# A layer kernel on one core: the side transfers of the first sweep move from SyncE's queue to GpSimd's, and the root of a block's rows from GpSimd to VectorE

## The chip, the cores and the metric

The kernel runs on one core of a Trainium2 chip. The metric is the device time of one execution in microseconds; of three executions the median counts: 2177.08 us (2176.64 to 2177.74). A second number is the span, from the first to the last instruction of one profiled execution.

## The reference

One layer over 4096 latent tokens of 1024 channels, with 256 context tokens ahead of them, all in float32:

```python
mod_lat = silu(c) @ w_mod + b_mod                 # shift, scale, gate
a_lat = rmsnorm(x, norm_g) * (1 + sc_l) + sh_l    # a_ctx likewise, from ctx and c_ctx
q, zf, zb, v, ga, u, ug, gb = split(a_lat @ w_in) # 8 groups of 512 columns
o   = hgrn2 forward(q, v, zf) + hgrn2 backward(q, v, zb)   # gated linear recurrence, 4 heads x 128
y   = silu(layernorm(conv31(u * sigmoid(ug)) + conv_b))    # half of it along rows, half along columns
out = concat(headnorm(o) * silu(ga), y * silu(gb)) @ w_out
result = rmsnorm(x + gt_l * out, final_norm_g)
```

f is lb + (1 - lb) * sigmoid(z), the key is 1 - f, and a state is S = f * S + k v^T per token. The states start from those at the end of the context.

## The kernel before, in words

The work goes through the tokens twice. The first sweep takes 16 blocks of 256 tokens in rising order: it projects q, zf, zb, v, u and ug, runs the forward recurrence and the convolution along rows, and stores what the backward recurrence needs. The second sweep goes down again and makes the gates, the convolution along columns, the backward recurrence and the output projection. The change is in the first sweep alone. Projections are done with float16 pairs, a high and a low half, in three passes of matmuls (PASSES), so TensorE has about 76 us of work in a block.

In a block `b` of the first sweep several generators are merged, each a sequence of steps: `hgrn` (the recurrence of the block), `row_conv`, the projections of this block and the next ones, `prep_rows` of block b+2, and the side work `side[b]` of blocks 1 to 11. The program's text gives the work in this merged order; a scheduler of the framework then sets the final order on each engine with a model of its own, so an edit in one place can move instructions elsewhere, and side work may stand in the block before the one that it is written for. Every engine takes its instructions in order: one that waits holds all behind it. The same holds for the DMAs that SyncE (SP) issues, and for those that GpSimd (POOL) issues.

`hgrn` in a block: five levels multiply keys and queries X by products of f (L763, L764 on VectorE), ScalarE copies km (L756), and TensorE makes the scores pl (L731). Then come two more growths, Q and H (L773, L774, each for two groups gi), with scores across (L784, L785). Then `split_keys` makes K: the high half on ScalarE (L560), the low half on VectorE (L561), and a DMA transpose of K into X on SP's queue (L562). There are two K buffers for four splits in a block. `keys_to_u` on TensorE reads the transposed keys (pu, L578); `forward` updates the state s_f (L583).

`prep_rows` of a block (two tiles of 128 rows): a load of x into xt (L258), the square sum on ScalarE (L261), L262, the root of the mean (`rsqrt`, L78 on VectorE, then L81 and three times L84 and L85 on GpSimd: L81 halves, each pair is one Newton step on a 128x1 tile), the scaling (L268, L270), the split in halves hl (L271 on ScalarE, L273 on VectorE), and two DMA transposes of hl into aT on SP's queue (L276).

The side work prepares the weights of the second sweep: `gate_rows` (loads wmt, L861), `scale_w2` (loads wst L885, squares L888), `split_w2` (load L897, halves L188 and L189, store of hl into w2d L900), `wo_scales` (loads L909, squares L911), `split_wo` (loads of gw L974 and L975, L979, halves L980 and L981, store of hl into wod L982). It shares its buffers with `prep_rows`: tag "xt" has two buffers, tag "A" (hl, junk, sqj, gacc) has one, so the halves of one piece of side work can't be written before the store, or the transposes, of the piece before have read theirs.

Of the kernel before, what the change touches and what calls it, by code (L numbers as in the profile page):

```python
# [19 lines left out]
P = 128  # L20
D = 1024
# [52 lines left out]
def rsqrt(nc, pool, out, v, n, tag, eng=None):  # L74

    eng = eng or nc.gpsimd
    y, t, h = out, pool.tile([P, n], F32, tag=tag + "t", name=tag + "t"), v
    nc.vector.tensor_scalar(y.bitcast(I32), v.bitcast(I32), -0.5, float(0x5F3759DF), ALU.mult, ALU.add)  # L78
    if n == 1:
        h = pool.tile([P, n], F32, tag=tag + "h", name=tag + "h")  # L80
        eng.tensor_scalar(h, v, -0.5, 0.0, ALU.mult, ALU.add)  # L81
    for _ in range(3):
        if n == 1:
            eng.tensor_scalar(t, y, y, h, ALU.mult, ALU.mult)  # L84
            eng.tensor_scalar(y, t, 1.5, y, ALU.add, ALU.mult)  # L85
        else:
            eng.tensor_tensor(t, y, y, ALU.mult)  # L87
            eng.tensor_tensor(t, t, v, ALU.mult)  # L88
            eng.tensor_scalar(t, t, -0.5, 1.5, ALU.mult, ALU.add)  # L89
            eng.tensor_tensor(y, y, t, ALU.mult)  # L90
# [8 lines left out]
def hymba_block(  # L99
# [3 lines left out]
    nc = tc.nc  # L103
    x, cx, out = x[0], cx[0], out[0]
    w_mod, w_in, w_out, conv_w = w_mod[0], w_in[0], w_out[0], conv_w[0]

    cp = ctx.enter_context(tc.tile_pool(name="cp", bufs=1))
    sm = ctx.enter_context(tc.tile_pool(name="sm", bufs=2))
# [33 lines left out]
    gtd = dr.tile([P, D], F32, tag="gtd", name="gtd")  # L142
    gsd = dr.tile([2, D], F32, tag="gsd", name="gsd")
    w2d = {g: [dr.tile([P, 2, 2 * 512], F16, tag=f"w2d{g}_{i}", name=f"w2d{g}_{i}") for i in range(4)] for g in (G_GA, G_GB)}
    wod = [dr.tile([P, 2, KC, 512], F16, tag=f"wod{n}", name=f"wod{n}") for n in range(2)]
# [20 lines left out]
    def group_scale(ssq, g):  # L166

        with tc.high_priority():
            tot = sm.tile([P, 1], F32, tag="tot", name="tot")
            nc.vector.tensor_reduce(tot, ssq, AX.X, ALU.add)  # L170
            pb = ps_lv.tile([P, 512], F32, tag="lv", name="pb")
            nc.tensor.matmul(pb[:, 0:1], ones, tot, start=True, stop=True)
            rw = rwall[:, g, :]
            tot2 = sm.tile([P, 1], F32, tag="tot2", name="tot2")
            nc.vector.tensor_copy(tot2, pb[:, 0:1])
            exponent(rw[:, 0:1], rw[:, 1:2], tot2)

    def evac_scale(g):
        for i in range(2):
            nc.vector.tensor_scalar(es[:, i, g : g + 1], rwall[:, g, 1:2], ra[:, i : i + 1], 2.0 ** -28, ALU.mult, ALU.mult)  # L180
# [10 lines left out]
    def win_rows(g, k, n):  # L191
        return w_in[k * P : (k + n) * P, 512 * g : 512 * g + 512].rearrange("(k p) n -> p k n", p=P)
# [4 lines left out]
    with ExitStack() as s1:  # L197
# [55 lines left out]
        def prep_rows(r0, aT):  # L253

            for i in range(2):
                t = e1.tile([P, D], F32, tag="xt", name="xt", bufs=2)
                hl = e1.tile([P, 2, D], F16, tag="A", name="hl")
                nc.sync.dma_start(t, x[r0 + i * P : r0 + (i + 1) * P, :])  # L258
                yield
                ssq = sm.tile([P, 1], F32, tag="xssq", name="xssq")  # L260
                nc.scalar.activation(hl[:, 0, :].bitcast(BF16), t, AF.Square, accum_out=ssq)  # L261
                nc.vector.tensor_scalar(ssq, ssq, 1.0 / D, EPS, ALU.mult, ALU.add)  # L262
                r = sm.tile([P, 1], F32, tag="xr", name="xr")
                rsqrt(nc, sm, r, ssq, 1, "xq")
                yield
                for sl in (slice(0, 512), slice(512, D)):
                    ts = t[:, sl]
                    nc.vector.scalar_tensor_tensor(ts, ts, r, gs[:, 0, sl], ALU.mult, ALU.mult)  # L268
                    yield
                    nc.vector.tensor_tensor(ts, ts, gs[:, 1, sl], ALU.add)  # L270
                    nc.scalar.copy(hl[:, 0, sl], ts)  # L271
                    yield
                    nc.vector.tensor_tensor(hl[:, 1, sl], ts, hl[:, 0, sl], ALU.subtract)  # L273
                    yield
                for j in range(2):
                    nc.sync.dma_start_transpose(aT[:, j, :, i * P : (i + 1) * P], hl[:, j, :])  # L276
# [105 lines left out]
        for r0, src in ((R_NG, norm_g[0]), (R_BM, b_mod[0]), (R_LB, lb_logits.rearrange("a b n -> (a b n)")),  # L382
                        (R_HG, hgrn_norm_g[0]), (R_CB, conv_b[0]), (R_LG, conv_ln_g[0]), (R_LBI, conv_ln_b[0])):
            n = src.shape[0] // P
# [471 lines left out]
        def gate_rows():  # L856

            acc = e1.tile([P, D], F32, tag="A", name="gacc")
            for k in range(KC):
                t = e1.tile([P, D], F32, tag="xt", name="wmt", bufs=2)  # L860
                nc.sync.dma_start(t, w_mod[k * P : (k + 1) * P, 2 * D : 3 * D])  # L861
                if k == 0:
                    nc.vector.tensor_scalar(acc, t, sc2[:, k, 0:1], None, ALU.mult)
                else:
                    nc.vector.scalar_tensor_tensor(acc, t, sc2[:, k, 0:1], acc, ALU.mult, ALU.add)
                yield
            bt = e1.tile([P, D], F32, tag="xt", name="bt", bufs=2)
            nc.sync.dma_start(bt, bass.AP(b_mod.tensor, b_mod.offset + 2 * D, [[0, P], [1, D]]))
            for j in range(2):
                sl = slice(512 * j, 512 * j + 512)  # L870
                pg = ps_o.tile([P, 512], F32, tag="o", name="pg")
                nc.tensor.matmul(pg, ones, acc[:, sl], start=True, stop=True)
                nc.vector.tensor_tensor(bt[:, sl], bt[:, sl], pg, ALU.add)
            nc.sync.dma_start(gtd, bt)
            nc.vector.tensor_reduce(gmx[:, 0:1], bt, AX.X, ALU.max)
            nc.vector.tensor_reduce(gmx[:, 1:2], bt, AX.X, ALU.min)
            yield

        def scale_w2(g):

            ssq = sm.tile([P, 8], F32, tag="ssq", name="ssq")
            for i in range(4):
                t = e1.tile([P, 2, 512], F32, tag="xt", name="wst", bufs=2)
                junk = e1.tile([P, 2, 512], BF16, tag="A", name="sqj")
                nc.sync.dma_start(t, win_rows(g, 2 * i, 2))  # L885
                yield
                yield
                nc.scalar.activation(junk, t, AF.Square, accum_out=ssq[:, i : i + 1])  # L888
                yield
            group_scale(ssq[:, 0:4], g)  # L890
            evac_scale(g)

        def split_w2(g, i):

            t = e1.tile([P, 2 * 512], F32, tag="xt", name="wst", bufs=2)
            hl = e1.tile([P, 2, 2 * 512], F16, tag="A", name="hl")
            nc.sync.dma_start(t.rearrange("p (k n) -> p k n", n=512), win_rows(g, 2 * i, 2))  # L897
            yield
            split_chunk(hl[:, 0, :], hl[:, 1, :], t, g)
            nc.sync.dma_start(w2d[g][i], hl)  # L900
            yield

        def wo_scales():

            ssq = sm.tile([P, 8], F32, tag="ssq", name="ssq")
            for k in range(KC):
                t = e1.tile([P, D], F32, tag="xt", name="wst", bufs=2)
                junk = e1.tile([P, D], BF16, tag="A", name="sqj")
                nc.sync.dma_start(t, w_out[k * P : (k + 1) * P, :])  # L909
                yield  # L910
                nc.scalar.activation(junk, t, AF.Square, accum_out=ssq[:, k : k + 1])  # L911
                yield
# [55 lines left out]
        def split_wo(k):  # L968

            for n in range(2):  # L970
                sl = slice(512 * n, 512 * n + 512)
                gw = e1.tile([P, 2, 512], F32, tag="xt", name="gw", bufs=2)
                hl = e1.tile([P, 2, 512], F16, tag="A", name="hl")
                nc.sync.dma_start(gw[:, 0, :], gtd[:, sl])  # L974
                nc.sync.dma_start(gw[:, 1, :], w_out[k * P : (k + 1) * P, sl])  # L975
                yield
                w = gw[:, 1, :]
                f = khg[:, k : k + 1] if k < 4 else kw[:, 1:2]
                nc.vector.scalar_tensor_tensor(w, w, f, gw[:, 0, :], ALU.mult, ALU.mult)  # L979
                nc.scalar.copy(hl[:, 0, :], w)  # L980
                nc.vector.tensor_tensor(hl[:, 1, :], w, hl[:, 0, :], ALU.subtract)  # L981
                nc.sync.dma_start(wod[n][:, :, k, :], hl)  # L982
                yield

        side = {1: [gate_rows()], 2: [scale_w2(G_GA), scale_w2(G_GB)]}
        for i in range(4):
            side[3 + i] = [split_w2(G_GA, i), split_w2(G_GB, i)]
            side[8 + i] = [split_wo(2 * i), split_wo(2 * i + 1)]
# [325 lines left out]
```

## Time and profile before

| | before |
|---|---|
| median of 3 executions | 2177.08 us |
| profiled execution, time | 2179.47 us |
| profiled execution, span | 2177.7 us |
| granted TensorE clock, mean | 0.981 |
| TensorE, VectorE, ScalarE, GpSimd busy | 2056.2, 1757.6, 1006.0, 371.6 us |
| side work's DMA issues on SP: wmt, bt, gtd, wst (in, out), w2d, gw (two), wod | 8, 1, 1, 16, 8, 8, 32, 16 |

The busy numbers are of the whole span. The first sweep's blocks lie between about 100 and 1410 us, and a block begins on a row of opd (the store of the forward result, L830). Block numbers below are those of the first opd row in a stretch: the stretch from 211.0 to 295.9 us holds what ends with the keys of block 1, the one to 375.5 those of block 2, and so on; block 12 ends at 1196.5. A wait in the trace is idle time of an engine, put down to what came last.

### The profile page before, as it was taken

Reading aid. Unit: us, or ns where it says so; the run is one execution under the profiler, and the core shown is the slowest. Engines: PE = TensorE matmul, PEld = TensorE weight load, DVE = VectorE, ACT = ScalarE, POOL = GpSimd, SP = SyncE. Lnnn points to the kernel's source line nnn. Section 1 sums busy time; section 2 is a strip of 40 time slices with the busy share of each in tenths; the row PEclk is TensorE's granted clock in tenths of the full one; section 3 lists DMA queues with packets and bytes.
Section 4 is the critical chain, followed back from the end, with each engine's and each line's share of the span. In section 5 each row is a group of like instructions: output and inputs, shape, how many; then the busy total and the mean of one; then the engine's idle time right before and its main releaser. Section 6 shows DMA issues by size and latency. Waiting matters only on the chain. (4 is left out here: it accounts for less than half of the span.)

```text
span 2177.7 us, 54464 instructions
## 1 busy us (share of the span) xinstructions
PE 2056.2 (94%) x22339; PEld 1517.2 (70%) x22339; DVE 1757.6 (81%) x4283; ACT 1006.0 (46%) x2326; POOL 371.6 (17%) x886
## 2 busy tenths in 40 slices
PE   6999999999998998999999999989999999999998
PEld 3777778778777887777788888655555555565664
DVE  5988877977975978978887975969999888888744
ACT  4944546445446445455445434433343333343343
POOL 1110101101101101101101100013433333333222
PEclk8999999999999999999999999989999999999999
DMA  9436155335235254253333225443332222333221
GB/s 363 136 90 161 60 151 161 69 113 130 71 113 144 74 145 138 63 161 114 74 108 63 52 55 156 152 155 102 107 107 93 97 98 92 120 120 115 97 78 59
DMA packets 222082, 247.96 MB, mean 114 GB/s; under 512 B 143652, under 2 KB 151672, under 8 KB 217864
## 3 DMA queue, kind: packets, MB, share of 16 engines
q1 hardware_dynamic: 221288, 240.19, 37.8%
q8 instruction: 175, 2.87, 0.6%
q0 software_dynamic: 544, 4.29, 0.5%
q14 instruction: 75, 0.61, 0.1%
HBM read 138.52 MB, written 72.36 MB: 97 GB/s over the span
## 5 line engine op out<-in xcount | busy, mean ns | idle before, releaser
L289 PEld LDWEIGHTS <-w 128*128 128x128 f16 x4704 | 456.2, 98 | 61.8 <-issue 3.6
L711 DVE SCALAR_TENSOR_TENSOR yr<-gu,convw,yr 128x224 f32<-128x224 f32 (+2 forms) x900 | 357.9, 445 | 0.0
L1116 DVE SCALAR_TENSOR_TENSOR ycs<-gu_all,convw,ycs 128x256 f32<-128x256 f32 (+2 forms) x828 | 345.3, 471 | 0.0
L289 PEld LDWEIGHTS <-pair 128*128 128x128 f16 x3168 | 308.2, 98 | 39.4 <-issue 0.6
L1220 PE MATMUL py<-wo,yh 128*128 128x512 f16 x1024 | 251.4, 381 | 2.9 <-ACT yh L1204 2.9
L289 PE MATMUL ps_z<-aT,pair 128*128 128x256 f16 x1632 | 190.8, 276 | 0.0
L289 PE MATMUL ps_z<-aT,w 128*128 128x256 f16 x1632 | 188.6, 274 | 1.9 <-DVE aT L247 1.4
L1083 PE MATMUL ps_gb<-aT,w 128*128 128x256 f16 x1536 | 187.7, 273 | 0.0
L81 POOL TENSOR_SCALAR xqh<-xssq 128x1 f32<-128x1 f32 x30 | 12.5, 416 | 1022.8 <-DVE xssq L262 1022.8
L300 PE MATMUL pv<-w,aT 128*128 128x512 f16 x816 | 184.4, 379 | 1.3 <-DVE gu L675 1.3
L1071 PE MATMUL ps_ga<-w,aT 128*128 128x512 f16 x768 | 182.1, 382 | 0.0
L289 PE MATMUL ps_u<-aT,w 128*128 128x256 f16 x1536 | 181.3, 274 | 0.2 <-ACT q L657 0.2
L756 ACT COPY km<-X 128x512 f32<-128x512 f32 x160 | 107.9, 675 | 156.1 <-DVE X L764 155.8
L289 PE MATMUL ps_g<-aT,w 128*128 128x256 f16 x1536 | 177.8, 273 | 0.6 <-ACT q L657 0.6
L1220 PEld LDWEIGHTS <-yh 128*128 128x128 f16 x1024 | 100.4, 98 | 108.5 <-ACT yh L1204 4.0
L289 PE MATMUL ps_q<-aT,pair 128*128 128x256 f16 x1536 | 173.3, 273 | 0.0
L1083 PEld LDWEIGHTS <-w 128*128 128x128 f16 x1536 | 150.1, 98 | 31.8
L300 PEld LDWEIGHTS <-aT 128*128 128x128 f16 x816 | 77.4, 98 | 88.2 <-issue 1.5
L1071 PEld LDWEIGHTS <-aT 128*128 128x128 f16 x768 | 75.5, 99 | 81.6 <-issue 2.5
L1220 PE MATMUL py<-wo,yl 128*128 128x512 f16 x512 | 129.6, 379 | 0.0
L1226 ACT ACTIVATE jk<-xr 128x512 bf16<-128x512 f32 x64 | 40.3, 629 | 184.7 <-DVE xr L1224 128.4
L319 ACT ACTIVATE f<-f,lbv,oml 128x128 f32<-128x128 f32 x272 | 112.9, 486 | 0.0
(308 smaller groups left out, 3301.5 us busy)
## 6 DMA issues: line engine op xcount, KB each, us to landing
xt<-in_x_dram SPq DMA_DIRECT2D x32, 512.0 KB, 4.3
xr<-in_x_dram SPq DMA_DIRECT2D x32, 512.0 KB, 3.6
out_dram<-xr SPq DMA_DIRECT2D x31, 512.0 KB, 2.6
aTd<-aT SPq DMA_DIRECT2D x14, 1024.0 KB, 5.1
aT<-aTd SPq DMA_DIRECT2D x14, 1024.0 KB, 5.2
wst<-in_w_in_dram SPq DMA_DIRECT2D x16, 512.0 KB, 4.3
qb<-qbd SPq DMA_DIRECT2D x32, 256.0 KB, 2.7
ub<-ubd SPq DMA_DIRECT2D x32, 256.0 KB, 2.7
```

The lines of the kernel that those rows point to most:

```text
L81: eng.tensor_scalar(h, v, -0.5, 0.0, ALU.mult, ALU.add)
L289: nc.tensor.matmul(ps[:, j, :], w[:, wi, k, (ct + j) * P : (ct + j + 1) * P], aT[:, ai, k, :], start=n == 0, stop=n == 23)
L300: nc.tensor.matmul(pv, aT[:, ai, k, i * P : (i + 1) * P], W[G_V][:, wi, k, :], start=n == 0, stop=n == 23)
L319: nc.scalar.activation(fa, fa, AF.Identity, scale=oml[:, d, ct + j : ct + j + 1], bias=lbv[:, d, ct + j : ct + j + 1])
L711: nc.vector.scalar_tensor_tensor(ar[i][:, :, lo:hi], gr[i][:, :, lo + dl : hi + dl], convw[:, i, j : j + 1], ar[i][:, :, lo:hi], ALU.mult, ...
L756: nc.scalar.copy(fap(km, 0, kd), fap(Xs[gi], 0, ks))
L1071: nc.tensor.matmul(ps, aT[:, ai, k, i * P : (i + 1) * P], Wa[:, wi, k, :], start=n == 0, stop=n == 23)
L1083: nc.tensor.matmul(ps[:, j, :], Wb[:, wi, k, (ct + j) * P : (ct + j + 1) * P], aT[:, ai, k, :], start=n == 0, stop=n == 23)
L1116: nc.vector.scalar_tensor_tensor(ya, gu_all[:, i, (lo + dl) * GW : (hi + dl) * GW], convw[:, 2 + i, j : j + 1], ya, ALU.mult, ALU.add)
L1220: nc.tensor.matmul(py, y[:, k // 4, k % 4, :], W2["o", nh][:, wi, k, :], start=n == 0, stop=n == 23)
L1226: nc.scalar.activation(junk, h[:, sl], AF.Square, accum_out=hs[:, nh : nh + 1])
```

## The change

The DMA issues of all side work go from `nc.sync` to `nc.gpsimd`, and the root in `prep_rows` is given VectorE as its engine. Buffers, generators and the merging stay as they are.

```diff
@@ prep_rows
-                rsqrt(nc, sm, r, ssq, 1, "xq")
+                rsqrt(nc, sm, r, ssq, 1, "xq", nc.vector)
@@ gate_rows (also bt and the store gtd)
-                nc.sync.dma_start(t, w_mod[k * P : (k + 1) * P, 2 * D : 3 * D])
+                nc.gpsimd.dma_start(t, w_mod[k * P : (k + 1) * P, 2 * D : 3 * D])
@@ scale_w2
-                nc.sync.dma_start(t, win_rows(g, 2 * i, 2))
+                nc.gpsimd.dma_start(t, win_rows(g, 2 * i, 2))
@@ split_w2 (also its load)
-            nc.sync.dma_start(w2d[g][i], hl)
+            nc.gpsimd.dma_start(w2d[g][i], hl)
@@ wo_scales
-                nc.sync.dma_start(t, w_out[k * P : (k + 1) * P, :])
+                nc.gpsimd.dma_start(t, w_out[k * P : (k + 1) * P, :])
@@ split_wo
-                nc.sync.dma_start(gw[:, 0, :], gtd[:, sl])
-                nc.sync.dma_start(gw[:, 1, :], w_out[k * P : (k + 1) * P, sl])
+                nc.gpsimd.dma_start(gw[:, 0, :], gtd[:, sl])
+                nc.gpsimd.dma_start(gw[:, 1, :], w_out[k * P : (k + 1) * P, sl])
...
-                nc.sync.dma_start(wod[n][:, :, k, :], hl)
+                nc.gpsimd.dma_start(wod[n][:, :, k, :], hl)
```

The function that the root calls takes the engine as its last argument:

```python
def rsqrt(nc, pool, out, v, n, tag, eng=None):
    eng = eng or nc.gpsimd
```

First place: VectorE at the end of block 4, from the Q growths (X with 16x32) over the two H growths (8x64) to the first key splits K; xt, xssq, xr and xqt belong to `prep_rows`. Before:

```order
801 L774 TENSOR_TENSOR X<-X,FL 128x16x32
802 L773 TENSOR_TENSOR X<-X,FL 128x16x32
803 L774 TENSOR_TENSOR X<-X,FL 128x16x32
804 L262 TENSOR_SCALAR xssq<-xssq 128x1
805 L78 TENSOR_SCALAR xr<-xssq 128x1
806 L773 TENSOR_TENSOR X<-X,FL 128x8x64
807 L774 TENSOR_TENSOR X<-X,FL 128x8x64
808 L268 SCALAR_TENSOR_TENSOR xt<-xt,xr,gs 128x512 x2
809 L773 TENSOR_TENSOR X<-X,FL 128x8x64
810 L774 TENSOR_TENSOR X<-X,FL 128x8x64
811 L270 TENSOR_TENSOR xt<-xt,gs 128x512
812 L561 SCALAR_TENSOR_TENSOR K<-X,K 128x512
```

The same place in the changed kernel, which begins with the second side split L189 of the block (before, both L189 stood ahead of the Q growths):

```order
915 L189 SCALAR_TENSOR_TENSOR hl<-wst,rwall,hl 128x1024
916 L773 TENSOR_TENSOR X<-X,FL 128x8x64
917 L774 TENSOR_TENSOR X<-X,FL 128x8x64
918 L773 TENSOR_TENSOR X<-X,FL 128x8x64
919 L774 TENSOR_TENSOR X<-X,FL 128x8x64
920 L561 SCALAR_TENSOR_TENSOR K<-X,K 128x512 x2
921 L262 TENSOR_SCALAR xssq<-xssq 128x1
922 L78 TENSOR_SCALAR xr<-xssq 128x1
923 L81 TENSOR_SCALAR xqh<-xssq 128x1
924 L84 TENSOR_SCALAR xqt<-xr,xqh 128x1
925 L85 TENSOR_SCALAR xr<-xqt,xr 128x1
926 L84 TENSOR_SCALAR xqt<-xr,xqh 128x1
```

The root with its L262 and the scaling L268 and L270 now stand behind the first two key splits instead of among the H growths, and one L189 has moved from ahead of the Q growths to behind them. Blocks 3 and 5 have the same move of L189 and the root. Of the four side pieces (L979 to L981) of a block, three in blocks 8 and 9 and two in block 10 move from ahead of the first key split to behind it.

Second place: ScalarE at the end of block 6, where the side work is squares of w_out (L911). From the second scores' copies (SC) to the key splits, before:

```order
434 L911 ACTIVATE sqj,ssq<-wst 128x1024 x2
435 L657 ACTIVATE q<-ps_q,es 128x256 x2
436 L911 ACTIVATE sqj,ssq<-wst 128x1024
437 L803 COPY SC<-pl 64x4x64 x3
438 L560 ACTIVATE K<-X 128x512
439 L803 COPY SC<-pl 64x4x64
440 L261 ACTIVATE hl,xssq<-xt 128x1024
441 L560 ACTIVATE K<-X 128x512 x2
```

And in the changed kernel:

```order
426 L911 ACTIVATE sqj,ssq<-wst 128x1024 x2
427 L657 ACTIVATE q<-ps_q,es 128x256 x2
428 L803 COPY SC<-pl 64x4x64 x3
429 L560 ACTIVATE K<-X 128x512
430 L803 COPY SC<-pl 64x4x64
431 L911 ACTIVATE sqj,ssq<-wst 128x1024
432 L560 ACTIVATE K<-X 128x512
433 L911 ACTIVATE sqj,ssq<-wst 128x1024
434 L560 ACTIVATE K<-X 128x512
```

One square less stands ahead of the first key split, and squares now stand between the splits, where L261 stood.

Third place: SP's queue at the end of block 6, before:

```order
157 L909 DMA wst<-in_w_out_dram 128x1024 x5
158 L258 DMA xt<-in_x_dram 128x1024
159 L811 DMA qbd_152<-X 128x512
160 L909 DMA wst<-in_w_out_dram 128x1024
161 L811 DMA qbd_153<-X 128x512
162 L562 DMA_TRANSPOSE X<-K 128x8x128 x4
163 L830 DMA opd_120<-osb 128x512
```

In the changed kernel:

```order
119 L1031 DMA aTd_100<-aT 128x4096
120 L811 DMA qbd_152<-X 128x512
121 L811 DMA qbd_153<-X 128x512
122 L562 DMA_TRANSPOSE X<-K 128x8x128 x2
123 L258 DMA xt<-in_x_dram 128x1024
124 L562 DMA_TRANSPOSE X<-K 128x8x128 x2
125 L830 DMA opd_120<-osb 128x512
```

The side loads have left the queue, as all 90 side transfers do, and the load of x has come to stand between the two pairs of key transposes.

## Rows read from the trace of the kernel before

**Rows 1.** Page, part 1: each engine's busy time, share and instructions.

```profile
PE 2056.2 (94%) x22339; PEld 1517.2 (70%) x22339; DVE 1757.6 (81%) x4283; ACT 1006.0 (46%) x2326; POOL 371.6 (17%) x886
```

**Rows 2.** Windows, blocks 1 to 10, then block 12: busy us (count), clock, DMA.

```profile
core 0: us, PE busy (x) PEld busy (x) DVE busy (x) ACT busy (x) POOL busy (x), PEclk, DMA share, GB/s
210.99:1043.90 832.91, 782.07 (x10876) 643.03 (x10874) 677.06 (x1589) 420.90 (x890) 86.61 (x147) 0.98 0.42 114
1120.59:1196.52 75.93, 75.93 (x1091) 62.97 (x1089) 64.39 (x150) 38.33 (x83) 7.75 (x14) 1.00 0.31 65
```

**Rows 3.** Waits of PE, 211 to 1044 us: us in total, times, longest us.

```profile
PE pu L578 <- DMA X<-K: 27.5, 8, 7.6
PE pl L731 <- ACT km L756: 14.2, 16, 1.7
```

**Rows 4.** Timeline of PE, key products: start us, us, line, op, [idle before <-releaser].

```profile
287.33 1.44 PE L578 MATMUL pu<-v,X 128*128 128x128 f16 x12 [4.51 <-DMA X<-K]
...
453.53 1.44 PE L578 MATMUL pu<-v,X 128*128 128x128 f16 x12 [3.36 <-DMA X<-K]
...
538.60 1.44 PE L578 MATMUL pu<-v,X 128*128 128x128 f16 x12 [3.17 <-DMA X<-K]
...
620.24 1.44 PE L578 MATMUL pu<-v,X 128*128 128x128 f16 x12 [3.16 <-DMA X<-K]
...
704.57 1.44 PE L578 MATMUL pu<-v,X 128*128 128x128 f16 x12 [7.64 <-DMA X<-K]
...
871.74 0.83 PE L578 MATMUL pu<-v,X 128*128 128x128 f16 x12 [1.73 <-DMA X<-K]
...
953.70 0.83 PE L578 MATMUL pu<-v,X 128*128 128x128 f16 x12 [0.47 <-DMA X<-K]
...
1038.55 0.83 PE L578 MATMUL pu<-v,X 128*128 128x128 f16 x12 [3.41 <-DMA X<-K]
```

**Rows 5.** Timeline of VectorE, block 4's end; same columns.

```profile
522.04 1.28 DVE L189 SCALAR_TENSOR_TENSOR hl<-wst,rwall,hl 128x1024 f16<-128x1024 f32 x1 [5.96 <-ACT hl L188]
527.48 0.15 DVE L262 TENSOR_SCALAR xssq<-xssq 128x1 f32<-128x1 f32 x1 [1.74 <-ACT hl L261]
...
531.26 1.42 DVE L268 SCALAR_TENSOR_TENSOR xt<-xt,xr,gs 128x512 f32<-128x512 f32 x2 [2.24 <-POOL xr L85]
533.79 0.68 DVE L270 TENSOR_TENSOR xt<-xt,gs 128x512 f32<-128x512 f32 x1
534.39 0.68 DVE L561 SCALAR_TENSOR_TENSOR K<-X,K 128x512 f16<-128x512 f32 x1
```

**Rows 6.** Timeline of ScalarE, block 6's end.

```profile
696.29 1.06 ACT L911 ACTIVATE sqj<-wst 128x1024 bf16<-128x1024 f32 x1 [1.54 <-DMA wst<-in_w_out_dram]
...
698.37 0.63 ACT L560 ACTIVATE K<-X 128x512 f16<-128x512 f32 x1
```

**Rows 7.** Waits of ScalarE and VectorE, 211 to 1044 us.

```profile
DVE xt L268 <- POOL xr L85: 23.0, 19, 2.2
ACT hl L980 <- DMA wod<-hl: 19.8, 7, 3.7
```

**Rows 8.** Timeline of VectorE, the span's end: the one root that VectorE does.

```profile
2171.30 0.14 DVE L81 TENSOR_SCALAR hrh<-hv 128x1 f32<-128x1 f32 x1
...
2173.15 1.42 DVE L1234 SCALAR_TENSOR_TENSOR xr<-xr,hr,fng 128x512 f32<-128x512 f32 x2
```

**Rows 9.** Timeline of GpSimd, a root of block 6's stretch.

```profile
663.94 1.86 POOL L84 TENSOR_SCALAR xqt<-xr,xqh 128x1 f32<-128x1 f32 x1
...
666.27 0.34 POOL L84 TENSOR_SCALAR xqt<-xr,xqh 128x1 f32<-128x1 f32 x1
```

**Rows 10.** DMA issues: out<-in, queue, count, KB each, median us to landing.

```profile
xr<-in_x_dram SPq DMA_DIRECT2D x32, 512.0 KB, 3.6
...
aT<-aTd SPq DMA_DIRECT2D x14, 1024.0 KB, 5.2
...
wo<-wod POOLq DMA_DIRECT2D x2, 2048.0 KB, 8.6
```

More of the change, by code (lines that the diff above doesn't have):

```diff
@@ L867, in gate_rows @@
             bt = e1.tile([P, D], F32, tag="xt", name="bt", bufs=2)
-            nc.sync.dma_start(bt, bass.AP(b_mod.tensor, b_mod.offset + 2 * D, [[0, P], [1, D]]))
+            nc.gpsimd.dma_start(bt, bass.AP(b_mod.tensor, b_mod.offset + 2 * D, [[0, P], [1, D]]))
             for j in range(2):
@@ L873, in gate_rows @@
                 nc.vector.tensor_tensor(bt[:, sl], bt[:, sl], pg, ALU.add)
-            nc.sync.dma_start(gtd, bt)
+            nc.gpsimd.dma_start(gtd, bt)
             nc.vector.tensor_reduce(gmx[:, 0:1], bt, AX.X, ALU.max)
@@ L896, in split_w2 @@
             hl = e1.tile([P, 2, 2 * 512], F16, tag="A", name="hl")
-            nc.sync.dma_start(t.rearrange("p (k n) -> p k n", n=512), win_rows(g, 2 * i, 2))
+            nc.gpsimd.dma_start(t.rearrange("p (k n) -> p k n", n=512), win_rows(g, 2 * i, 2))
             yield
             split_chunk(hl[:, 0, :], hl[:, 1, :], t, g)
-            nc.sync.dma_start(w2d[g][i], hl)
+            nc.gpsimd.dma_start(w2d[g][i], hl)
             yield
```

## Prediction, made before the changed kernel ran

> **What bounds the kernel now.** I read the busy line of the page first: TensorE is busy for 2056.2 us, 94% of the span, and no other engine comes near it [rows 1]. So only TensorE's idle time and its pace are open to a change. The second view is the table of windows. It sets ten blocks with side work (1 to 10) beside block 12, which has none: block 12 takes 75.93 us, in all of which TensorE is busy at a granted clock of 1.00, while the ten take 832.91 us with 782.07 us busy at 0.98 [rows 2]. Ten blocks like block 12 would take 759.3 us. The excess, 73.6 us, is what the side work costs now. Of it 832.91 - 782.07 = 50.8 us is idle time of TensorE, and 2% of 832.91, that is 16.7 us, is a clock below its higher level of 2.4 GHz (1.00) for part of the time; the remaining 6 us are the side work's own matmuls and rounding.
>
> The third view says for whom TensorE waits there: 27.5 us in eight waits for the transposed keys (pu behind the DMA X<-K), and 14.2 us in sixteen small waits for km from ScalarE [rows 3]. The rest is in smaller groups. The timeline has the eight waits one by one: 3.36, 3.17 and 3.16 us in blocks 3 to 5, 7.64 us in block 6, 4.51 us in block 1, and 1.73, 0.47 and 3.41 us in blocks 8 to 10 [rows 4]. Such a wait means that the key splits K, and hence their transposes, came late at a block's end. What came ahead of them on VectorE in block 4 is to be read in the fourth view: L262 after 1.74 us of waiting for the square sum, L268 (1.42 us) after 2.24 us of waiting for the root on GpSimd, L270 (0.68 us), and only then K at 534.39 [rows 5]. On ScalarE in block 6 it is a square of w_out that waited 1.54 us for its load and took 1.06 us [rows 6].
>
> **The change part by part.** The order of the changed program moves more than the diff says, and I cost what moves.
>
> Part 1, blocks 3 to 5. L262, the root, L268 and L270 no longer stand ahead of the first two key splits on VectorE. In block 4 that takes 1.74 + 0.15 + 2.24 + 1.42 + 0.68 = 6.2 us out of K's way [rows 5], more than the 3.17 us that TensorE waits there. One L189 comes in between the Q and the H growths with its wait for ScalarE; before, it waited 5.96 us ahead of all the growths [rows 5], so the four Q growths now run inside that wait. The K waits of blocks 3, 4 and 5 all go: 3.36 + 3.17 + 3.16 = 9.7 us [rows 4]. Late next is ScalarE's own half of K, which is done some microseconds ahead of VectorE's in block 4, so nothing of the 9.7 comes back there.
>
> Part 2, block 6. One square and its wait leave the place ahead of ScalarE's first key split at 698.37: 1.54 + 1.06 = 2.6 of the 7.64 us [rows 6, 4]. The squares now between the splits keep the rest.
>
> Part 3, blocks 8 to 10. Three, three and two of four side pieces move behind the first key split. Ahead of it they made ScalarE wait for the store of the piece before: 19.8 us in seven waits, up to 3.7 us each [rows 7]. I take three quarters of 1.73 + 0.47 + 3.41 = 5.61 us, which is 4.2 us [rows 4]. In block 1 the root now stands densely between Q and H growths, ahead of the keys: I give nothing there. Keys together: 9.7 + 2.6 + 4.2 = 16.5 of 27.5 us.
>
> Part 4, the clock. The stretch without waits has 1.00, that with them 0.98 [rows 2]. I let the 16.7 us shrink with the waits: 16.7 x 16.5 / 27.5 = 10.0 us. Between nothing and 16.7 this is the proportional value.
>
> Part 5, the root on VectorE. Before, VectorE waited 23.0 us in nineteen waits for it, 1.21 us each [rows 7]. The only root that VectorE makes before runs from 2171.30 to 2173.15, so 1.85 us for seven small instructions [rows 8]. If the wait was on the path and the root's time is nowhere on it, a root gives back 1.21 us; if the wait was covered and VectorE's time is on the path, it costs 1.85. Twenty roots in blocks 1 to 10 at the difference, 0.64 us, are 12.8 us of VectorE. VectorE is busy 677.06 of 832.91 us [rows 2], so most of that lies in its idle time. I let four blocks in ten pay it, since TensorE waits for a growth's km in about that share of them, and charge +5 us. The bounds are 20 x 0.4 x 1.85 = +15 and 20 x 0.4 x (-1.21) = -10 us.
>
> Part 6, the queue. Ninety transfers of the side work leave SP's queue for GpSimd's, which did few before. SP's rows give 3.6 us to landing for 512 KB and 5.2 for 1024 KB, so 1.6 us for each further 512 KB; 2048 KB would come to 8.4 us there, and GpSimd's two transfers of that size took 8.6 [rows 10]. On this a transfer costs 0.2 us more on GpSimd. But these two are no transfers in a busy sweep. There GpSimd's own work can be stretched: the same 128x1 operation took 1.86 us once and 0.34 us the next time, 1.52 us more [rows 9]. If the issue suffers likewise, each transfer costs up to 1.52 us more. The other end is a gain: SP's queue no longer makes key transposes, loads of x and stores stand behind a side transfer that waits for its buffer. Two transfers of a block, a load and the store that frees the single buffer A, lie in a chain to the keys. Twenty of them at 0.2 us are 4 us, half of it covered: +2. I stay near the lower value because it comes from transfers on that very queue.
>
> The sum is -16.5 - 10.0 + 5 + 2 = -19.5 us. The profiled execution took 2179.47 us, so it would become 2160.0; that execution lies 2.4 us above the median of 2177.08, and on the median's scale the forecast is 2158 us.
>
> **Rivals.**
>
> Everything goes. If the keys are never late any more and the clock stays up, the change wins 27.5 + 16.7 = 44.2 us [rows 2, 3] and the median becomes 2133. For it: the side transfers are out of SP's way in every block, not only at the places that I counted. Against: block 6 still has squares between its splits, and block 1's root stands ahead of the keys. Chance 0.13.
>
> No change. Buffers stay as they are: a piece of side work still waits until the store of the piece before has read A, whichever queue issues it, and the waits of 19.8 us [rows 7] may only change their place. Then keys and clock gain nothing, the root lies between -10 and +15 with the most weight near zero, and the time is 2177, within 4.4 us either way. Those 4.4 us, 0.2%, are about what a measurement of this kernel can tell from no change. In this case the change does not do what it says: the queue gets empty, but nothing had waited for the queue. Chance 0.15. The Trainium skill, "DMA: Bandwidth & Descriptors", section "Issuing engines are not separate DMA queues", speaks for this: it says that transfers of all issuers run interleaved on the same 16 DMA engines, and that spreading them saves the issuing time alone. By this rule my parts 1 to 3 would have to come from the moved instructions only; no row here shows two issuers in the same stretch.
>
> Slower: GpSimd issues late. While VectorE works, operations on GpSimd stretch by 1.52 us [rows 9], and VectorE is busy 81% of the ten blocks [rows 2]. If each issue is held like that, the two chained transfers of a block come 1.52 us later, 20 x 1.52 = 30.4 us. Half is covered, as in part 6, and 15 us remain; the keys and the clock are then not better than before, and the root adds its 5. The time is 2177 + 20 = 2197, or 2212 if nothing is covered. The place is the load and the store of hl at L188 and L980 ahead of the key splits. The case decides once the two transfers of a block cost more than about 1.3 us each in full, since 20 x 1.3 outweighs the 26.5 of parts 1 to 4. Against it: the 0.2 us of the large transfers [rows 10]. Chance 0.25. The Trainium skill, "SBUF — State Buffer", section "SBUF: two separate sides", gives a cause: descriptors of transfers issued from GpSimd are written by its cores, which a VectorE operation in a two-port mode locks out; its advice is to issue from SP or ScalarE. Its example, some 620 ns grown to 3100, would make an estimate of 2.5 us a transfer and 25 us for the twenty, half covered, so 2207 with the root; no trace of before shows an issue of GpSimd among VectorE's growths.
>
> **How the numbers follow.** The likeliest case, 0.47, is 2158, with a range of its own from 2145 (the root at its lower bound, -10, brings 2143; some of that is shared with part 1) to 2168 (the root at +15). Everything goes 0.13, no change 0.15, slower 0.25. From these, faster has 0.47 + 0.13 = 0.60. The range from 2129 to 2192 holds the first three cases and the near part of the slower one; outside lie most of the slower case, about 0.16, and a sliver below.
>
> **What would show it right or wrong.** The wait of pu for X<-K in blocks 1 to 10 should fall from 27.5 to about 11 us, with those of blocks 3 to 5 gone and block 6 near 5. The ten blocks should take about 812 us instead of 832.91, and the clock there lie between 0.98 and 1.00. VectorE's wait at L268 for GpSimd has to vanish, with L81 to L85 of the first sweep in VectorE's rows at some 0.2 to 0.3 us each. Part 5 is wrong if the wait of pl for km grows past 14.2 us by more than 5, or falls. Part 6 is wrong if the side loads and stores land later on GpSimd's queue by 1 us or more than they did on SP's, and if ScalarE's waits at L188 and L980 for the store of hl grow. If the keys still come late by 25 us, the forecast as a whole has failed, wherever the time ends.

## The result: slower by 1.4%

The changed kernel takes 2208.69 us (median; 2203.82 to 2211.43), before 2176.87 us. The ratio is 1.0143, with a 95% interval from 1.0124 to 1.0161. The forecast was 2158 us, faster; the time lies beyond the upper end of the range, 2192 us.

The profile after begins with the busy line, which answers to [rows 1]:

```profile
PE 2061.8 (93%) x22339; PEld 1518.7 (69%) x22339; DVE 1785.9 (81%) x4493; ACT 1004.2 (46%) x2326; POOL 292.3 (13%) x766
```

TensorE has the same instructions and is busy for 5.6 us more, so the other 23 us of the longer span (2206.6 against 2177.7 us) are idle time. The windows of blocks 1 to 10 and of block 12, columns as in [rows 2]:

```profile
213.40:1077.30 863.90, 787.01 (x10842) 642.61 (x10840) 697.60 (x1732) 416.23 (x885) 49.49 (x82) 0.97 0.43 110
1160.38:1236.18 75.80, 75.80 (x1089) 62.83 (x1087) 66.80 (x166) 37.94 (x83) 0.00 (x0) 1.00 0.27 65
```

Block 12, without side work, is as it was (75.80 against 75.93 us). The ten blocks take 863.90 instead of 832.91 us, and block 11 takes 83.08 instead of 76.69; from block 12 on, the profiled execution is 10.9 us shorter than before, for a cause that stays open. So the loss lies in blocks 1 to 11, where side work runs. It is not spread evenly: blocks 1 to 3 lose 9.2 us together, blocks 4 to 7 only 1.0, and blocks 8 to 11 lose 27.2. The windows of blocks 4, 8 and 10, first before and then after:

```profile
460.51:543.35 82.84, 78.78 (x1100) 65.23 (x1098) 66.46 (x152) 40.77 (x85) 8.88 (x14) 0.98 0.39 107
790.06:877.15 87.09, 78.65 (x1100) 63.99 (x1098) 74.41 (x168) 43.65 (x94) 10.90 (x21) 1.00 0.51 145
959.60:1043.90 84.30, 76.89 (x1072) 63.03 (x1072) 68.62 (x159) 40.55 (x88) 8.35 (x14) 0.98 0.41 114
```

```profile
472.12:555.83 83.71, 77.75 (x1074) 63.82 (x1073) 69.70 (x170) 40.54 (x86) 2.56 (x4) 0.96 0.38 105
802.66:897.51 94.85, 83.46 (x1105) 67.96 (x1102) 75.12 (x179) 41.50 (x89) 11.32 (x19) 0.93 0.46 117
981.20:1077.30 96.10, 81.07 (x1095) 65.27 (x1094) 72.09 (x175) 40.89 (x88) 7.79 (x13) 0.96 0.46 107
```

TensorE's waits in the ten blocks (total, times, longest), against [rows 3]:

```profile
PE pu L578 <- DMA X<-K: 32.6, 8, 7.8
PE pl L731 <- ACT km L756: 19.0, 17, 3.8
PE pl L784 <- DVE X L774: 7.3, 5, 4.0
PE pu L578 <- DVE xqt L84: 4.1, 1, 4.1
```

The keys were to be waited for 11 us and are waited for 32.6 us. The last row belongs to them too: the matmul reads no xqt, and the keys' transposes were landing then. The single waits of blocks 3, 4, 5 and 6, against [rows 4]:

```profile
468.03 0.83 PE L578 MATMUL pu<-v,X 128*128 128x128 f16 x12 [3.53 <-DMA X<-K]
...
550.12 1.44 PE L578 MATMUL pu<-v,X 128*128 128x128 f16 x12 [4.06 <-DVE xqt L84]
...
633.12 1.44 PE L578 MATMUL pu<-v,X 128*128 128x128 f16 x12 [4.93 <-DMA X<-K]
...
719.44 1.44 PE L578 MATMUL pu<-v,X 128*128 128x128 f16 x12 [7.83 <-DMA X<-K]
```

None of them got shorter. How the change works on the keys is to be read in the merged timeline of block 4's end, which answers to [rows 5] (SP's row merges two issues and gives the start of the first):

```profile
532.79 1.28 DVE L189 SCALAR_TENSOR_TENSOR hl<-wst,rwall,hl 128x1024 f16<-128x1024 f32 x1 [5.65 <-ACT hl L188]
534.11 8.51 SPq L258 DMA_DIRECT2D xt<-in_x_dram  x2
534.38 0.56 POOL L900 DMA_DIRECT2D w2d<-hl  x1 [7.76 <-DVE hl L189]
...
539.79 1.15 ACT L188 ACTIVATE hl<-wst,rwall 128x1024 f16<-128x1024 f32 x1 [3.18 <-DMA w2d<-hl]
...
540.98 1.28 DVE L189 SCALAR_TENSOR_TENSOR hl<-wst,rwall,hl 128x1024 f16<-128x1024 f32 x1 [4.49 <-ACT hl L188]
...
542.55 0.56 POOL L900 DMA_DIRECT2D w2d<-hl  x1 [7.62 <-DVE hl L189]
...
544.59 1.29 DVE L561 SCALAR_TENSOR_TENSOR K<-X,K 128x512 f16<-128x512 f32 x2
```

The moves of the order are there: K stands right behind the growths, and L262 and the root behind it. But L189 ends, and in the next third of a microsecond two transfers start: SP's load of x into the buffer that L189 has read, and GpSimd's store of hl. Buffer A is free only when that store has landed, so the next L188 begins 5.4 us after the store's issue, and VectorE waits for it with the H growths behind. From the first K split to the matmul it is then 550.12 - 544.59 = 5.5 us, before 538.60 - 534.39 = 4.2 us [rows 4, 5]: the keys' transposes run beside the second store. Block 4 as a whole loses only 0.9 us by this.

In block 8, which loses 7.8 us, the rows ahead of the key products are these, before:

```profile
867.27 9.25 SPq L562 DMA_TRANSPOSE X<-K  x4
```

and after:

```profile
882.65 0.68 POOL L982 DMA_DIRECT2D wod<-hl  x1 [6.46 <-DVE hl L981]
883.23 0.66 POOL L974 DMA_DIRECT2D gw<-gtd  x1
883.77 0.65 POOL L975 DMA_DIRECT2D gw<-in_w_out_dram  x1
883.99 12.81 SPq L562 DMA_TRANSPOSE X<-K  x4
891.13 1.44 PE L578 MATMUL pu<-v,X 128*128 128x128 f16 x12 [5.47 <-DMA X<-K]
```

The first key transposes need 891.13 - 883.99 = 7.1 us to the matmul, where they needed 871.74 - 867.27 = 4.5 [rows 4]. GpSimd has just issued a store and two loads of the side work. That these are what slows the transposes is a reading; no run tests it.

The side transfers' times to landing over the whole run (KB each, median us), first before and then after:

```profile
wst<-in_w_in_dram SPq DMA_DIRECT2D x16, 512.0 KB, 4.3
w2d<-hl SPq DMA_DIRECT2D x8, 512.0 KB, 3.2
gw<-in_w_out_dram SPq DMA_DIRECT2D x16, 256.0 KB, 3.5
wod<-hl SPq DMA_DIRECT2D x16, 256.0 KB, 3.0
```

```profile
wst<-in_w_in_dram POOLq DMA_DIRECT2D x16, 512.0 KB, 5.1
w2d<-hl POOLq DMA_DIRECT2D x8, 512.0 KB, 5.5
gw<-in_w_out_dram POOLq DMA_DIRECT2D x16, 256.0 KB, 5.6
wod<-hl POOLq DMA_DIRECT2D x16, 256.0 KB, 4.6
```

In the changed kernel they land 0.8 to 2.3 us later from GpSimd's queue; the prediction had 0.2.

### The profile page after: what moved, and what is told of

The parts are those of the page before. It is cut to its first block, busy times and chain, and to the rows that moved or that the text cites. A ratio compares the mean times of both kernels' runs of the same rounds, so it can differ in the third digit from the quotient of the medians.

```text
span 2206.6 us, 54499 instructions
## 1 busy us (share of the span) xinstructions
PE 2061.8 (93%) x22339; PEld 1518.7 (69%) x22339; DVE 1785.9 (81%) x4493; ACT 1004.2 (46%) x2326; POOL 292.3 (13%) x766
## 5 line engine op out<-in xcount | busy, mean ns | idle before, releaser
L711 DVE SCALAR_TENSOR_TENSOR yr<-gu,convw,yr 128x224 f32<-128x224 f32 (+2 forms) x900 | 366.1, 447 | 0.0
L578 PE MATMUL pu<-v,X 128*128 128x128 f16 x816 | 63.0, 227 | 55.6 <-DMA X<-K 37.7
```

The costliest lines, as they stand in the source:

```text
L578: nc.tensor.matmul(pu[:, hd, :], K[:, ki, hd, :], V[:, vi, hd * P : (hd + 1) * P], start=n == 0, stop=n == 2)
L711: nc.vector.scalar_tensor_tensor(ar[i][:, :, lo:hi], gr[i][:, :, lo + dl : hi + dl], convw[:, i, j : j + 1], ar[i][:, :, lo:hi], ALU.mult, ...
```

## The experiments

### The two parts apart

```diff
 # e1: kernel before, and
+rsqrt(nc, sm, r, ssq, 1, "xq", nc.vector)
 # e2: kernel before, and all side transfers
+nc.gpsimd.dma_start(...)
```

> Only the root of prep_rows goes to VectorE; all side transfers stay on SP's queue. Theory Q (the queue costs the 32 us): 2177 us, within 6, since the root's wait of 23.0 us at L268 goes and 20 roots of 1.85 us come to VectorE, which has idle time. Theory R (the root on VectorE and the order that it brings cost the 32 us): 2200 us or more, with the level waits pl<-km well above 14.2 us.

> Only the side transfers go to GpSimd's queue; the root stays on GpSimd. Theory Q: 2203 us or more, with key transposes X<-K landing at 4.5 us or later instead of 3.4, and ScalarE waiting for aT<-hl and wod<-hl as in the changed kernel. Theory R: 2177 us within 6, or faster. If both parts cost about half, this and the run of the root alone come to some 2190 each.

The root alone is faster: 2164.62 us, ratio 0.9943 (0.9923 to 0.9963). The queue alone is slower: 2202.02 us, 1.0123 (1.0098 to 1.0148). So the queue is what turns the change into a loss. The parts don't add up: +27 and -12 us alone, but +32 together. The gain of the root, which neither theory expected, does not show once the queue is added: the changed kernel is not faster than the queue alone. Why it doesn't is not settled.

Theory Q came within 1 us of the time, but its sign did not show: with the queue alone the key transposes land at 4.2 us, not 4.5 or later, and TensorE waits 26.8 us for the keys in the ten blocks, no more than the 27.5 of before. What grew there is its wait for the scores across (pl at L784, for the growth L774 on VectorE), 11.3 us for 3.4, with small waits beside it. Each such growth stands right behind an operation of VectorE that had waited 4.8 to 6.8 us for what ScalarE writes into A (L189, L981, L262 or L170). So it is the same chain through A, and it reaches TensorE by the scores here.

### Loads and stores apart

```diff
 # e3: root on GpSimd, stores gtd, w2d, wod on SP, side loads:
+nc.gpsimd.dma_start(...)
 # e4: root on GpSimd, side loads on SP, stores:
+nc.gpsimd.dma_start(w2d[g][i], hl)     # and wod, gtd
```

> Root on GpSimd; only the side loads (wmt, bt, wst, gw) go to GpSimd's queue, the stores (gtd, w2d, wod) stay on SP's. Theory Q1 (the loads start as soon as a buffer of xt is free, which is when the transposes of hl run, and slow them): most of what the queue costs, 2195 us or more, and aT<-hl with long landings of 8 us or more. Theory Q2 (the store that frees A lands later from GpSimd): little, 2177 to 2183 us.

> Root on GpSimd; only the stores of the side work (gtd, w2d, wod) go to GpSimd's queue, the loads stay on SP's. Theory Q2 (the store lands 1.6 to 2.3 us later and holds the single buffer A): most of what the queue costs, 24 stores at about 1.5 us on the path in part, 2190 us or more. Theory Q1 (the loads collide with the transposes): 2177 us within 5.

Loads alone 2195.36 us, 1.0089 (1.0068 to 1.0110); stores alone 2197.53 us, 1.0101 (1.0074 to 1.0127). Either half costs most of what both cost, so neither theory stands alone, and the halves don't add up. With the stores back on SP, w2d lands at 2.9 us; with only the stores on GpSimd, at 5.7.

### The halves of split_wo out of buffer A

```diff
-hl = e1.tile([P, 2, 512], F16, tag="A", name="hl")
+hl = gw[:, 0, :].bitcast(F16).rearrange("p (a n) -> p a n", a=2)
```

> The root on VectorE, all side transfers on SP, and in split_wo the halves hl are written over the half of gw that is used up, so that blocks 7 to 10 no longer need buffer A for the side work. Theory A (ScalarE's waits at L980 for the store wod<-hl, 21.6 us, and for aT<-hl, 9.8 us, of the run with the root alone hold the keys there): 8 to 15 us less than the root alone, 2150 to 2157 us. Rival (these waits only fill ScalarE's idle time, and gw is now held by the store instead): 2165 us within 5.

> The side transfers on GpSimd, the root on GpSimd, and hl of split_wo in gw's place, so that its store holds a buffer of gw, not A. Theory A (GpSimd's later landing costs through the single buffer A): the blocks of split_wo get back what they lost against before, some 11 us of the 27, so 2190 us or less. Rival (the cost comes through the loads, the order, or the longer hold of gw): 2197 to 2210 us.

With the root on VectorE: 2155.70 us, 0.9899 (0.9872 to 0.9925), so 21 us better than before: the version that beats both, some 9 us below the root alone, with intervals that just touch. With the queue: 2192.68 us, 1.0065 (1.0042 to 1.0088), so some 9 us of the 27 back by the medians and 13 by the ratios; the 2190 us expected were just missed. In this run wod lands at 2.9 us from GpSimd, as from SP (3.0), and not at 4.1 as with the queue alone: its store now holds the buffer that L981 used to free, so no load can start into it beside the store. Both runs fit theory A, that the single buffer is part of the path; the order moves with the edit too, and these runs don't tell the two apart.

### The same with the order held nearly fixed

The timeline model moves hundreds of instructions for any edit. With it off, the order is nearer to the text, all is slower, and an edit moves less.

```diff
-with _tile.TileContext(nc, schedule_with_timeline_sim=True) as tc:
+with _tile.TileContext(nc, schedule_with_timeline_sim=False) as tc:
```

> The kernel before, with the framework's scheduling by its timeline model switched off: the basis for the next run, where the same switch is set. No theory gives its time; it is asked only that the next run be set against it. More than 2177 us is likely, since the order is then nearer to the program's text.

> The run before with the side transfers on GpSimd and nothing else. The order on the engines then moves little: 16 rows of some 28,000 on TensorE and 269 on VectorE differ, where with the timeline model 707 and 969 do. Theory L (GpSimd's later landings cost by themselves): 12 to 30 us above the run before. Theory O (the order that the scheduler makes of it costs): within 6 us of the run before.

2359.39 us for the plain kernel before and 2443.05 us with the queue: 84 us more. Theory O is out, and theory L had the direction, but its 12 to 30 us were far too small. So GpSimd's queue costs without the timeline model too; how much of the 27 us in the scheduler's order comes from the order is not shown by this. The root, which shares GpSimd's queue with issues that wait, is not what costs here: VectorE waits for it at L268 for 48.9 us in 21 waits between 211 and 1250 us, and waited 51.2 us in 22 before. The two runs can be set side by side, and the order is the same on most rows but not on all: in the block whose keys come at 495 us in the plain kernel before, the root stands ahead of the key splits once the queue is moved. One pair of split_w2 pieces in the plain kernel before, merged timeline:

```profile
562.80 0.32 SPq L900 DMA_DIRECT2D w2d<-hl  x1
563.17 1.11 SPq L258 DMA_DIRECT2D xt<-in_x_dram  x1
566.74 1.15 ACT L188 ACTIVATE hl<-wst,rwall 128x1024 f16<-128x1024 f32 x1 [1.78 <-DMA w2d<-hl]
...
569.23 0.32 SPq L900 DMA_DIRECT2D w2d<-hl  x1
...
572.21 1.06 ACT L261 ACTIVATE hl<-xt 128x1024 bf16<-128x1024 f32 x1 [0.47 <-DMA w2d<-hl]
```

The same with the queue alone:

```profile
584.65 8.90 SPq L258 DMA_DIRECT2D xt<-in_x_dram  x2
584.92 0.58 POOL L900 DMA_DIRECT2D w2d<-hl  x1 [6.74 <-DVE hl L189]
590.73 1.15 ACT L188 ACTIVATE hl<-wst,rwall 128x1024 f16<-128x1024 f32 x1 [3.92 <-DMA w2d<-hl]
...
593.49 0.56 POOL L900 DMA_DIRECT2D w2d<-hl  x1 [7.98 <-DVE hl L189]
599.15 1.06 ACT L261 ACTIVATE hl<-xt 128x1024 bf16<-128x1024 f32 x1 [3.42 <-DMA w2d<-hl]
```

From the first store to the next use of A it was 566.74 - 562.80 = 3.9 us and is 5.8; from the second 3.0 and 5.7. That is 4.6 us on one chain in one block. On SP's queue the load of x stood behind the store; on two queues it starts ahead of it.

### ScalarE's queue, and squares in place

```diff
 # e9: side transfers, root on GpSimd
+nc.scalar.dma_start(...)
 # e10: e5, and in scale_w2 and wo_scales
-nc.scalar.activation(junk, t, AF.Square, ...)
+nc.scalar.activation(t, t, AF.Square, ...)
```

> The side transfers go to ScalarE's queue instead of GpSimd's; the root stays on GpSimd. Theory G (the late landing belongs to issues from GpSimd): w2d<-hl lands in about 3.2 us as from SP, not 5.5 to 6.0, and the time is 2177 us within 10, unless ScalarE is held by issues that wait for a buffer. Theory S (any second queue beside SP's lands late, since the transfers then run beside the transposes): w2d<-hl at 5 us or more and 2195 us or more.

> The run with the root on VectorE and split_wo in place, and in addition the squares of scale_w2 and wo_scales written over their own input, so that buffer A serves the side work only in gate_rows and split_w2. Theory A (waiting for A at the squares, 5 to 11 us in all, is on the path in blocks 1, 2, 5 and 6): 3 to 8 us less than the 2155.7 of that run. Rival (it lies beside other work): 2156 us within 4.

From ScalarE it is 2198.69 us, 1.0113 (1.0088 to 1.0139), no better than GpSimd. There w2d lands at 5.2 us as well, while wst lands as from SP (4.2 to 4.3 us) and gw from w_out a little later (4.1 for 3.5 us). So a late store is not GpSimd's alone. The time itself is not clean, since ScalarE is held by issues that wait for VectorE. The squares bring nothing more: 2157.98 us, 0.9929 (0.9904 to 0.9953), as the rival said.

### The root in the plain order

> Scheduling by the timeline model off, transfers on SP, only the root on VectorE, to be set against 2359.4 us. Theory W (the root's wait at L268, 51.2 us in 22 waits there, stands on the chain to the keys): 10 to 30 us less. Theory O (the gain of the root alone, 12 us, came from the order that the scheduler made of it): 2359 us within 6.

> Scheduling by the timeline model off, both parts of the change, to be set against 2443.0 us of the queue alone. If the two parts add up, it differs from that run by as much as the root alone differs from 2359.4 us. Rival (with the transfers late, the root no longer matters, as the changed kernel's 2208.7 us beside the queue alone at 2202.0 suggests): 2443 us within 8.

The root alone gives 2317.64 us, 42 us less than 2359.39, and with the queue 2379.53 us, 64 us less than 2443.05. So most of VectorE's 51.2 us of waiting for GpSimd's root stood on the path. Theory W's direction holds; its size was too small. With the queue the root is worth more, not the same and not nothing, so neither of the two expectations for that run holds; why it is worth more is not settled. In the scheduler's order it was worth 12 us alone and nothing with the queue.

### The load of x on the same queue

```diff
 # e13: e8; e14: e2; e15: e7; in prep_rows
-nc.sync.dma_start(t, x[r0 + i * P : r0 + (i + 1) * P, :])
+nc.gpsimd.dma_start(t, x[r0 + i * P : r0 + (i + 1) * P, :])
 # e16: e7, side transfers
+nc.scalar.dma_start(...)
```

> Scheduling by the timeline model off, side transfers on GpSimd and the load of x (L258) there too, so that it stands behind the store of hl again; the order on TensorE and ScalarE is the same as with the side transfers alone. Theory S (store and load of x run beside each other on two queues): w2d<-hl lands in 3.7 us or less instead of 5.6, and the time falls from 2443.0 us by 20 us or more. Theory G (issuing from GpSimd is what is late): w2d<-hl stays above 5 us and the time is 2443 us within 8, or more, since the loads of x are late then too.

> The same with the timeline model on, root on GpSimd, to be set against the 2202.0 us of the side transfers alone. Theory S: 8 to 20 us less, 2182 to 2194 us. Theory G: 2202 us within 6, or more.

> Timeline model off; all side transfers stay on SP, only the load of x goes to GpSimd. Theory S: the store from SP now runs beside the load of x, so w2d<-hl lands at 4.5 us or later though SP issues it (3.4 us with both on SP), and the time is 15 us or more above 2359.4. Theory G: the stores land as before, and the time is 2359 us within 8, since a load of x is needed long after it lands.

> Timeline model off, side transfers on ScalarE's queue, root on GpSimd. Theory S: w2d<-hl at 4.5 us or later and 2410 us or more, near GpSimd's 2443.0. Theory G: w2d<-hl at 3.4 us and below 2390 us, what is above 2359.4 being ScalarE's own issues.

The plain queue with the load of x behind the store (e13), merged timeline:

```profile
588.78 0.57 POOL L900 DMA_DIRECT2D w2d<-hl  x1 [7.60 <-DVE hl L189]
589.35 0.55 POOL L258 DMA_DIRECT2D xt<-in_x_dram  x1
592.82 1.15 ACT L188 ACTIVATE hl<-wst,rwall 128x1024 f16<-128x1024 f32 x1 [2.15 <-issue]
```

Now 4.0 us pass from store to use, as on SP, though GpSimd issues. The median landing of w2d is 3.5 us, against 5.6 in e8; from ScalarE with x's load on SP (e16) it is 6.6, from the only two landings of eight that this trace has. Between e8 and e13 the order on ScalarE is the same, and on VectorE it is but for a few rows ahead of these blocks. So the store's delay is the load of x beside it, not the engine that issues it. The times are told by stretches. These are windows (columns as in [rows 2]) of three stretches with split_w2 and of the four with split_wo, in the plain kernel before, with the queue (e8), with the queue and x (e13), and from ScalarE (e16):

```profile
413.00:678.50 265.50, 237.74 (x3266) 193.76 (x3264) 204.22 (x460) 122.22 (x257) 13.03 (x46) 0.96 0.35 99
852.70:1213.50 360.80, 321.87 (x4339) 259.84 (x4337) 278.64 (x632) 163.08 (x350) 22.05 (x63) 0.95 0.38 106
```

```profile
422.30:716.00 293.70, 246.34 (x3265) 198.72 (x3264) 205.28 (x464) 122.14 (x257) 22.47 (x61) 0.92 0.34 89
893.80:1296.60 402.80, 328.38 (x4354) 263.91 (x4353) 280.23 (x637) 162.60 (x350) 46.89 (x104) 0.92 0.38 95
```

```profile
434.20:710.90 276.70, 243.83 (x3266) 196.81 (x3265) 203.82 (x460) 122.14 (x257) 23.67 (x61) 0.94 0.35 95
887.00:1284.20 397.20, 330.82 (x4352) 264.57 (x4350) 280.27 (x638) 162.91 (x350) 52.46 (x115) 0.93 0.38 97
```

```profile
415.20:692.60 277.40, 238.65 (x3265) 194.28 (x3264) 204.06 (x462) 123.48 (x259) 14.07 (x49) 0.94 0.34 93
867.20:1248.80 381.60, 326.38 (x4332) 261.64 (x4330) 280.19 (x633) 162.84 (x351) 21.72 (x63) 0.94 0.37 100
```

In the split_w2 stretches GpSimd's queue costs 28.2 us, and 11.2 once x's load stands behind the store: 17 us were the two transfers side by side. Part of the 11.2 may be the order, which is not that of e7 in one of the three blocks. In the split_wo stretches it costs 42.0 and still 36.4. There each piece needs its loads too, and gw from w_out lands at 3.7 us from SP, 4.3 from ScalarE, 5.2 and 5.5 from GpSimd; ScalarE's queue costs 20.8 there. ScalarE's 11.9 us in the split_w2 stretches are no measure of a late store, since its order is another: the key splits stand 1.8 us behind L261 in e16 (587.29 after 585.49) and 6.1 in e7 (578.32 after 572.21). As a whole e13 takes 2430.34 us, 13 less than e8, between the two theories' numbers, and e16 takes 2386.94 us, so 28 above e7 where GpSimd is 84 above. Its store is late as theory S said, and its time is below 2390 us as theory G said. Theory S is shown for the stores of split_w2. For the rest the later landing of loads from GpSimd (theory G) is a candidate; it is not shown, since the order of e7 and e8 differs in the split_wo blocks.

Two further expectations failed. With x's load alone on GpSimd (e15, 2373.74 us, 14 more than e7), SP's store still lands at 3.2 us in the median: there the store is issued first (569.66 against 569.93 us in the block looked at), and what comes first is not slowed. The one store of that run which the load of x preceded, at 409.28 us behind 408.91, took 6.1 us to land, the longest, though SP issued it. And in the scheduler's order (e14) the store lands at 3.9 instead of 6.0 us, yet the time is 2205.33 us, 1.0159 (1.0139 to 1.0178), where 8 to 20 us were to come back. The loads of x land later (5.0 for 4.2 us) and the order moves; which of these ate the gain was not settled. So in the scheduler's order, which is that of the change, no run shows what the store beside the load of x costs; blocks 4 to 6, where it is seen, lose 3 us in the changed kernel.

## Why the prediction was wrong

What bounds the kernel was read rightly: blocks with side work lose, by key waits and a lower clock, and block 12 has nothing to lose.

Part 6 is the step that failed. It priced a transfer on GpSimd's queue at 0.2 us more, from two transfers of 2048 KB that run when next to nothing else is in flight [rows 10], and charged +2 us. The queue alone measured +27 us, with landings 1.1 to 2.8 us later (wod 4.1, w2d 6.0 us), and in the changed kernel 0.8 to 2.3. The row was of the right engine and of the wrong situation: here the transfers are small, and they start on the very event that starts another on SP's queue. The gain that the part set against it, a free SP queue, turned round. SP's queue had been an order of precedence: the store that frees A went first and the load of x, needed much later, behind it. The Trainium skill, "DMA: Bandwidth & Descriptors", section "Issuing engines are not separate DMA queues", says that transfers of all issuers interleave on the same engines. The trace agrees (3.4 us alone in its turn, 5.6 to 6.6 beside the load of x), and I used the page only for a rival without effect.

Parts 1 to 3 took the key waits to fall by 16.5 us. They rose instead: 32.6 us for 27.5, and in blocks 8 to 10, where part 3 gave 4.2 us back, 13.3 us for 5.6. The instructions moved as described, but L262 and the root were not what came last ahead of the K splits. Ahead of them stands a serial chain through A: the transposes of hl, the first piece with its store, then the second piece. The store in it became longer, and the step "the four Q growths now run inside that wait" gave the H growths to a wait of 4.5 us for the second piece. Late next was not ScalarE's half of K but this chain. Part 4, the clock, followed the keys the wrong way: 0.97 for 0.98, and 0.93 for 1.00 in block 8. How the 27 us that blocks 8 to 11 lose divide between landings, key transposes and order stays open.

Part 5 had the wrong sign. The root alone, in the scheduler's order, gains 12 us where +5 was charged; the wait for GpSimd was on the path. The measured gain lies a little beyond its lower bound, -10. In the changed kernel this gain is not seen.

The rival "GpSimd issues late" gave 2197 to 2212 us and held 0.25; the measured 2208.7 lies in it. Its place was right, the load and the store at L188 and L980, and its size per transfer, 1.52 us, lies within the 0.8 to 2.3 measured. That its sum came out is in part luck: it charged all ten blocks alike, and 5 us for a root that gains by itself. Its cause is not borne out for the stores. The store lands in 3.5 us from GpSimd while VectorE works as before, so the stretching of GpSimd's operations by VectorE [rows 9] does not explain the stores. Nor do GpSimd's issues show it: each side transfer's own instruction took 0.53 to 0.79 us in the changed kernel, in e8 and in e13, never 1.5 us more. For the loads, most of which stay about 1 us late with either arrangement, the cause stays open: no run here took VectorE's work away.

## What to carry to other kernels

One DMA queue is also an order of precedence, as the plain order shows: before a transfer is moved to a second queue, look which transfers start on the same event, and which of them frees a buffer on the critical path. A price for a transfer is taken from one of its size in a busy stretch, not from a lone large one. A change of two parts is to be costed and run in its parts; here one gained 0.6% and the other lost 1.2%, and together they lost 1.4%.

## What the runs showed of the hardware

- A 512 KB store (w2d) took 2.9 to 4.2 us to land, in the median of a run, where its queue sent it ahead of the load of x, from SP (before, e1, e3, e7, e15) or from GpSimd (e13, e14). It took 5.2 to 6.6 us where that 512 KB load mostly started at the same time or up to 0.4 us ahead on SP's queue and the store came from GpSimd (the changed kernel, e2, e4, e8, e12) or from ScalarE (e9, e16).
- The loads of 256 KB (gw from w_out) landed in the plain order at 3.7 us from SP (e7), 4.3 from ScalarE (e16) and 5.2 from GpSimd (e8); those of 512 KB from w_in (wst) at 4.3, 4.4 and 5.2 us. Those of 512 KB from w_out took 5.0, 5.0 and 4.9 us, so not every load lands later from GpSimd.
- GpSimd's instruction for a side transfer of 256 or 512 KB took 0.53 to 0.79 us in each case (the changed kernel, e8, e13), while VectorE was busy for 81% of the ten blocks of the changed kernel.
